# The HGRN loop of a two-layer diffusion backbone, regrouped into a two-stage pipeline over heads

## Chip, cores and metric

One core of a Trainium2 chip runs the whole kernel. The metric is device time in microseconds: the time before is the median of three runs, 1417.72 us (1417.47 to 1418.39). A profiled execution of the same kernel is the source of every duration below.

## What is computed

The reference is a two-layer backbone on 512 latent tokens of width 1024, with 256 context tokens. Layer 0 mixes tokens with a gated linear recurrence in two directions (HGRN2), layer 1 with a short convolution; each is followed by a squared-ReLU MLP. The part that the change touches is the recurrence, in 8 heads of 128 channels:

```python
parts = split(h @ w_in, 5)                 # forget gates of two directions, value, query, output gate
f = lb + (1 - lb) * sigmoid(parts[d])      # per direction d;  k = 1 - f,  g = log f
cum = cumsum(g)                            # within chunks of 64 tokens
o_inter = (q * exp(cum)) @ S
scores = tril((q * exp(cum - ref)) @ (k * exp(ref - cum)).T)
o = o_inter + scores @ v
S = exp(last) * S + (k * exp(last - cum)).T @ v     # the first S comes from the context tokens
y = rmsnorm(o_dir0 + o_dir1) * gnorm * silu(gate)
```

All of it is float32. A matrix product of the layers is made of three products of rounded halves (high with high, high with low, low with high).

## The kernel before

Channels lie on the partitions and tokens along the rows, 512 wide. Weights come in blocks of 1024 by 256, each in two halves (`load_half`): SP's queue loads a half, ScalarE rounds it (`whi`, L316), VectorE makes the rest (`wlo`, L317). Three such halves fit at a time (pool `wa`). One head goes through these steps:

- **Forget products** (`forget_steps`, `block_steps`, tile `ps_fl`): 48 matmuls of 512 columns for the two directions' gates of the latent tokens; 48 of 256 columns for the context tokens (`context_products`, `ps_fc`).
- **Gates** (`forget_gates`, `latent_sigmoid`, `context_sigmoid`): sigmoids on ScalarE into `k` and `kc`, and on VectorE a copy of the products plus a bias, `zb` (L737).
- **Operands** (`logs`, `latent_ops`): logarithms and exponentials on ScalarE, scans along the tokens and products on VectorE. They give the scaled keys and queries of both directions and the scaled context keys `kc`.
- **Recurrence** (`context_states`, `states`, `scores`, `recurrence`): transposes, context states (`ctr`, `cst`), states (`ktr`, `kv`, `S`), masked scores (`sc`, `scm`, `scs`) and the output `po`, then the sum of squares `oms`. These are short matmuls, each waiting for ScalarE or VectorE between steps.
- **Readout** (`readout`): output gate and normalisation into `yT`.

Two heads share the query block (`silu_steps(3, ...)`, tile `ps_p`), the output gate block (`p4`, also `ps_p`) and the value block (`value_products`, `psv`), each of the same size as a forget block or, for the values, 144 matmuls of 256 columns.

The loop goes over pairs of heads, A and B. In a pair the order of the text is: operands of A, values, recurrence of A, operands of B, gate block, recurrence of B. While a recurrence runs, an object `Fill` puts matmuls of the next forget block (or of the query block, or in the last head of the first half of the output projection, `out_steps`, `ps_woa`) between its short matmuls; the table `GAPS` says for each head how many go into each of seven gaps. `Fill.step` fixes the order of these matmuls on TensorE. So the operands of a head are made right ahead of its recurrence, and the products that stand in the text between them (values, gate block, the rest of a block) are what TensorE has meanwhile.

A scheduler places each instruction on its engine when its simulated inputs are ready, first by the order of the text; each engine then runs its list in order. `tables.switch` keeps the activations that need one ScalarE table together: sigmoids of one group, then logarithms and exponentials (`LOGEXP`), then sigmoids again. Product banks of PSUM: four for `mm_tile` (`ps_fl`, `ps_fc`, `ps_p`, `psv`, `ps_woa`), three for the short matmuls (`sm_tile`), one for `po` and `oms`.

`tick()` takes two of the 24 units of the layer's other modulation vectors: each unit is a load of 512 KB on SP's queue into one of two buffers and one VectorE step of 128 by 1024 (`acc`, L442, L444); every eighth ends with a rounding (`alo`, L455) and two matmuls (`adaps`). `tick` is called up to five times a pair, from the second pair on.

Before the last recurrence, `y_split` rounds the finished heads 0 to 3 (`y_hi`, `y_lo`, L229, L230), which `out_steps` multiplies.

Of the kernel before, what the change touches and what calls it, by code (L numbers as in the profile page):

```python
# [46 lines left out]
def dit_kernel(ctx, tc, x, c, ctx_in, c_ctx, ada_w, ada_b, norm1, norm2, norm_f, mlp_w1, mlp_w2,  # L47
# [309 lines left out]
    class Fill:  # L357


        def __init__(self, hd, *steps):  # L360
            self.gaps, self.steps, self.ins = iter(GAPS[hd]), steps, None

        def gap(self):

            n = next(self.gaps)
            for steps in self.steps:
                for ins in itertools.islice(steps, n):
                    self.step(ins)
                    n -= 1
# [7 lines left out]
        def finish(self, i=0):  # L377

            for _ in self.steps[i]:
                pass  # L380
# [260 lines left out]
    def context_sigmoid(z, hd):  # L641
        kc = ht("kc", f"kc_{hd}", 2 * CTX, 1)
        act_fn(kc, z, AF.Sigmoid)
        return kc

    def logs(zs, hd):
# [6 lines left out]
        for d in range(2):  # L653
            kk, z = zs[d][1]
            g = ht("g", f"g_{hd}_{d}", SEQ + 2, 2)
# [6 lines left out]
        for d in range(2):  # L662
# [4 lines left out]
            c_ = ht("c64", f"c64_{name}", SEQ, 3)  # L667
# [16 lines left out]
            e1 = ht("de", f"e1_{name}", SEQ, 4)  # L684
# [29 lines left out]
    def context_states(kc, hd, vc, fill):  # L714

        ps = sm_tile(f"ctr_{hd}")
        for t in range(4):
            ins = nc.tensor.transpose(ps[:, t * P:(t + 1) * P], kc[:, t * P:(t + 1) * P], ident)
            fill.step(ins)
            pins.setdefault(f"ctr{hd}", ins)  # L720
        fill.gap()
        kT = ht("kT", f"kcT_{hd}", 2 * CTX, 2)
        nc.scalar.copy(kT, ps)
        ps2 = sm_tile(f"cst_{hd}")
        for d in range(2):
            for t in range(2):
# [48 lines left out]
    def states(o, d, s0, v, name, fill):  # L775
        order = list(range(4) if d == 0 else range(3, -1, -1))
        ps = sm_tile(f"ktr_{name}")
        for i, n in enumerate(order[:3]):
            fill.step(nc.tensor.transpose(ps[:, i * P:(i + 1) * P], o["kp"][:, n * P:(n + 1) * P], ident))
# [15 lines left out]
    def recurrence(hd, ops, s0, v, fill):  # L795

        S = []
        for d in range(2):
            S.append(states(ops[d], d, s0[d], v, f"{hd}_{d}", fill))
            if d:  # L800
                fill.gap()
# [458 lines left out]
```

## Time and profile before

| | us |
|---|---|
| median of the runs | 1417.72 |
| profiled execution, its own time | 1422.73 |
| its span in the trace | 1420.8 |
| TensorE busy in the span | 1361.4 |
| VectorE busy | 910.9 |
| ScalarE busy | 578.7 |

In the trace PE is TensorE's matmul row and PEld its row of weight loads, DVE is VectorE, ACT ScalarE, POOL GpSimd, SP the queue that loads weights. L316 is line 316 of the kernel. Matmuls overlap each other, so one's duration is longer than the distance from its start to the next one's; that distance, here called the pitch, is what a matmul costs in a row of them. PEclk is the granted clock of TensorE as a share of 2.4 GHz; it takes two levels, 1.0 and 0.5 (1.2 GHz).

### The profile page before, as it was taken

To read this page: it belongs to the slowest core of one execution; us is meant where nothing else is said; L and a number is where in the kernel's file an instruction comes from. 1 tells how busy PE (TensorE), PEld (TensorE's weight loads), DVE (VectorE), ACT (ScalarE), POOL (GpSimd) and SP (SyncE) were. 2 spreads that over 40 slices of the span, in tenths; PEclk is the share of its full clock that TensorE was granted. 3 is DMA by queue.
4 is the path that set the end of the run, shared out by engine and by line. 5 is a ranking of instruction groups with operands and counts; after the bars stand their busy time and mean duration, and the time that the engine had idled before them with its cause. 6 is when DMAs were issued, how large, how long until landed. Compare 5 with 4: busy or idle time off the path is not lost.

```text
span 1420.8 us, 18668 instructions
## 1 busy us (share of the span) xinstructions
PE 1361.4 (96%) x7418; PEld 1162.3 (82%) x7418; DVE 910.9 (64%) x1378; ACT 578.7 (41%) x877; POOL 78.9 (6%) x87
## 2 busy tenths in 40 slices
PE   6998999999996989999999999999999999999997
PEld 4797897978885888888888889888889888888887
DVE  5695987878769697676565547544578544444536
ACT  6573447336545354242342434322244323132333
POOL 3000000000000210000000002000030100000000
PEclk9999999999997999999999999999999999999999
DMA  9713214423211316566555331333334532323211
GB/s 267 210 45 119 90 45 119 134 90 104 75 51 54 106 58 237 193 193 222 177 170 173 104 103 61 106 102 95 98 104 134 178 104 89 100 93 103 91 59 60
DMA packets 142267, 167.60 MB, mean 118 GB/s; under 512 B 6692, under 2 KB 121572, under 8 KB 142180
## 3 DMA queue, kind: packets, MB, share of 16 engines
q1 hardware_dynamic: 140964, 164.70, 36.4%
q0 software_dynamic: 1088, 1.65, 0.6%
q8 instruction: 58, 0.95, 0.3%
q14 instruction: 29, 0.24, 0.0%
q10 hardware_dynamic: 128, 0.05, 0.0%
HBM read 164.25 MB, written 2.14 MB: 117 GB/s over the span
## 4 chain that ended last, share of the span: by engine, by line
PE 76%; DVE 16%; DMA 3%; ACT 2%; issue 2%; SPq 0%; POOL 0%; DVEq 0%; ACTq 0%
PE ps_w L340 22%; PE ps_w L343 11%; PE ps_w2t L1199 4%; PE ps_w2t L1197 4%; PE ps_w2t L1198 4%; PE ps_fl L340 2%; DMA ada<-in_ada_w_dram 2%; PE ps_cvb L340 2%; PE ps_cwo L340 2%; PE ps_cvx L340 2%; PE ps_cvc L340 2%; PE ps_fc L340 1%; PE ps_p L340 1%; PE ps_fl L343 1%; PE ps_cvb L343 1%
## 5 line engine op out<-in xcount | busy, mean ns | idle before, releaser
L316 ACT CAST whi_w<-raw_w 128x1024 fp32r<-128x1024 f32 x128 | 134.2, 1053 | 279.3 <-PE ps_w L340 150.5
L317 DVE TENSOR_TENSOR wlo_w<-raw_w,whi_w 128x1024 fp32r<-128x1024 f32 x116 | 141.4, 1223 | 161.3 <-ACT whi_w L316 160.9
L340 PE MATMUL ps_w<-h_a_hi,whi_w 128*128 128x512 f32 (+1 forms) x576 | 207.5, 367 | 2.5 <-ACT h_a_hi L232 2.5
L340 PE MATMUL ps_w<-h_a_lo,whi_w 128*128 128x512 f32 x448 | 174.3, 389 | 0.0
L340 PEld LDWEIGHTS ps_w<-h_a_hi,whi_w 128*128 128x128 f32 x576 | 108.5, 188 | 21.1 <-ACT h_a_hi L232 2.9
L444 DVE SCALAR_TENSOR_TENSOR acc<-ada,cs,acc 128x1024 f32<-128x1024 f32 x70 | 89.8, 1283 | 49.0 <-DMA ada<-in_ada_w_dram 48.9
L343 PE MATMUL ps_w<-h_a_hi,wlo_w 128*128 128x512 f32 x448 | 119.7, 389 | 0.0
L1197 PE MATMUL ps_w2t<-whi_w,u_hi 128*128 128x512 f32 (+1 forms) x288 | 105.3, 366 | 0.0
L1198 PE MATMUL ps_w2t<-wlo_w,u_hi 128*128 128x512 f32 (+1 forms) x288 | 105.3, 366 | 0.0
L1199 PE MATMUL ps_w2t<-whi_w,u_lo 128*128 128x512 f32 (+1 forms) x288 | 105.2, 365 | 0.0
L340 PE MATMUL ps_w<-u_lo,whi_w 128*128 128x512 f32 (+1 forms) x288 | 103.3, 366 | 0.7 <-DVE u_lo L1069 0.7
L340 PE MATMUL ps_w<-u_hi,whi_w 128*128 128x512 f32 (+1 forms) x288 | 103.4, 366 | 0.0
L343 PEld LDWEIGHTS ps_w<-h_a_hi,wlo_w 128*128 128x128 f32 x448 | 84.1, 188 | 17.5
L340 PEld LDWEIGHTS ps_w<-h_a_lo,whi_w 128*128 128x128 f32 x448 | 84.1, 188 | 17.5
L1068 DVE TENSOR_TENSOR mr<-mr 128x512 f32<-128x512 f32 (+1 forms) x72 | 45.0, 630 | 45.5 <-ACT u_hi L1067 45.5
L1066 ACT ACTIVATE mr<-ps_w 128x512 f32<-128x512 f32 (+1 forms) x72 | 39.2, 545 | 80.0 <-PE ps_w L343 80.0
L343 PE MATMUL ps_w<-u_hi,wlo_w 128*128 128x512 f32 (+1 forms) x288 | 70.2, 365 | 0.0
L340 PEld LDWEIGHTS ps_w<-u_lo,whi_w 128*128 128x128 f32 x288 | 54.3, 189 | 10.0 <-DVE u_lo L1069 1.2
L340 PEld LDWEIGHTS ps_w<-u_hi,whi_w 128*128 128x128 f32 x288 | 54.3, 189 | 9.1
L1199 PEld LDWEIGHTS ps_w2t<-whi_w,u_lo 128*128 128x128 f32 x288 | 54.3, 189 | 8.8 <-issue 0.2
L1198 PEld LDWEIGHTS ps_w2t<-wlo_w,u_hi 128*128 128x128 f32 x288 | 54.3, 189 | 8.8
L1197 PEld LDWEIGHTS ps_w2t<-whi_w,u_hi 128*128 128x128 f32 x288 | 54.3, 189 | 8.7
(374 smaller groups left out, 3103.7 us busy)
## 6 DMA issues: line engine op xcount, KB each, us to landing
raw_w<-in_mlp_w_dram SPq DMA_DIRECT2D x128, 512.0 KB, 3.8
ada<-in_ada_w_dram SPq DMA_DIRECT2D x80, 512.0 KB, 4.7
adaw<-in_ada_w_dram SPq DMA_DIRECT2D x32, 256.0 KB, 5.5
raw_f<-in_hgrn_w_in_dram SPq DMA_DIRECT2D x32, 256.0 KB, 4.0
raw_p<-in_hgrn_w_in_dram SPq DMA_DIRECT2D x12, 512.0 KB, 3.5
raw_v<-in_hgrn_w_in_dram SPq DMA_DIRECT2D x8, 512.0 KB, 4.1
raw_cvb<-in_conv_w_in_dram SPq DMA_DIRECT2D x8, 512.0 KB, 3.6
raw_cwo<-in_conv_w_out_dram SPq DMA_DIRECT2D x8, 512.0 KB, 3.4
```

What stands on the lines that cost most here:

```text
L316: pins[name] = nc.scalar.copy(hi, raw)
L317: eng.tensor_tensor(out=lo, in0=raw, in1=hi, op=ALU.subtract)
L340: yield nc.tensor.matmul(ps, lhsT=w[i][:, k % KH, ms], rhs=rhs[k][j][:, c0:c1], start=(k == first and (i, j) == (0, 0)), stop=False)
L343: yield nc.tensor.matmul(ps, lhsT=w[late[0]][:, k % KH, ms], rhs=rhs[k][late[1]][:, c0:c1], start=False, stop=(k == last))
L444: ins = nc.vector.scalar_tensor_tensor(out=acc, in0=raw[:, 0, :], scalar=cs[:, j, 0:1], in1=acc, op0=ALU.mult, op1=ALU.add)
L1066: nc.scalar.activation(r, ps, AF.Relu)
L1068: nc.vector.tensor_tensor(out=r, in0=r, in1=r, op=ALU.mult)
L1197: nc.tensor.matmul(ps, lhsT=u[k][0][:, tk], rhs=whi[:, kk, c0:c1], start=(k == 0), stop=False)
L1198: nc.tensor.matmul(ps, lhsT=u[k][0][:, tk], rhs=wlo[:, kk, c0:c1], start=False, stop=False)
L1199: nc.tensor.matmul(ps, lhsT=u[k][1][:, tk], rhs=whi[:, kk, c0:c1], start=False, stop=(k == KT - 1))
```

## The change

- The loop goes over heads instead of pairs. In the text, the recurrence of head h comes first with the forget products of head h+2 as its fill (latent and context products, both through `Fill` now), then the operands of head h+1, then the gates of head h+2. Behind the fill stand the query block (even h) or the values (odd h) of the next pair.
- The output gate blocks of pairs 1 to 3 are kept back: two of them are the fill of head 6, the third follows it. The gate of a head is then multiplied into `yT` after its normalisation (`gate_y`).
- Ahead of the loop stand the operands of head 0, the forget products of head 1 and the values of pair 0.
- `GAPS` is one row of five lengths in microseconds for all heads; a matmul of 512 columns counts 0.227, one of 256 counts 0.118. In a recurrence all transposes come first, then the context states, both directions' states, then the scores.
- `zb` and the scaling of `k` are made by ScalarE (Identity with a per-partition bias, or scale and bias) instead of VectorE.
- `kl` and `ql` are written over `k`. Buffers: `g` 4 instead of 2, `k` 4 instead of 3, `c64` 4 instead of 3, `kc` 2 instead of 1, `de` is split into `qt` (3) and `kt` (4). The scratch for GpSimd's DMAs is set to 4096 bytes.
- `tick(2)` (four units) is called once a head, from head 0 on. The readout of head h-1 stands after the scores of head h, ahead of their sum `scs`.

```diff
-GAPS = ((0, 9, 4, 6, 5, 18, 9),
-        (66, 9, 5, 6, 4, 6, 0),
-        (0, 9, 4, 6, 2, 12, 12),
-        (22, 20, 10, 6, 4, 14, 18),
-        (0, 9, 9, 6, 2, 12, 14),
-        (18, 24, 5, 10, 6, 19, 14),
-        (0, 9, 4, 6, 2, 12, 12),
-        (30, 20, 4, 6, 4, 18, 7))
+GAPS = (3.2, 2.4, 2.4, 3.6, 4.6)
...
+        def __init__(self, *steps):
+            self.steps, self.ins = itertools.chain(*steps), None
+
+        def gap(self, us):
+
+            while us > 0:
+                got = next(self.steps, None)
+                if got is None:
+                    return
+                self.step(got[0])
+                us -= got[1]
...
-        kc = ht("kc", f"kc_{hd}", 2 * CTX, 1)
+        kc = ht("kc", f"kc_{hd}", 2 * CTX, 2)
...
-            g = ht("g", f"g_{hd}_{d}", SEQ + 2, 2)
+            g = ht("g", f"g_{hd}_{d}", SEQ + 2, 4)
...
-            c_ = ht("c64", f"c64_{name}", SEQ, 3)
+            c_ = ht("c64", f"c64_{name}", SEQ, 4)
...
-            e1 = ht("de", f"e1_{name}", SEQ, 4)
+            e1 = ht("qt", f"e1_{name}", SEQ, 3)
...
-            nc.vector.tensor_scalar(out=r["kk"], in0=r["kk"], scalar1=col(lb1n, d, hd), scalar2=col(lb1, d, hd),
-                                    op0=ALU.mult, op1=ALU.add)
+            nc.scalar.activation(r["kk"], r["kk"], AF.Identity, scale=col(lb1n, d, hd), bias=col(lb1, d, hd))
...
-        kk = ht("k", f"k_{hd}_{d}", SEQ, 3)
+        kk = ht("k", f"k_{hd}_{d}", SEQ, 4)
         act_fn(kk, z, AF.Sigmoid)
-        zb = ht("de", f"zb_{hd}_{d}", SEQ, 4)
-        nc.vector.tensor_scalar(out=zb, in0=z, scalar1=col(lbig, d, hd), scalar2=None, op0=ALU.add)
+        zb = ht("kt", f"zb_{hd}_{d}", SEQ, 4)
+        nc.scalar.activation(zb, z, AF.Identity, bias=col(lbig, d, hd))
...
+    def recurrence(hd, ops, kc, v, vc, fill, between):
+        orders = [list(range(4)), list(range(3, -1, -1))]
+        ps = sm_tile(f"ctr_{hd}")
+        for t in range(4):
+            fill.step(nc.tensor.transpose(ps[:, t * P:(t + 1) * P], kc[:, t * P:(t + 1) * P], ident))
+        kcT = ht("kcT", f"kcT_{hd}", 2 * CTX, 1)
+        nc.scalar.copy(kcT, ps)
+        kT = []
+        for d in range(2):
+            ps = sm_tile(f"ktr_{hd}_{d}")[:, 0:3 * P]
+            for i, n in enumerate(orders[d][:3]):
+                fill.step(nc.tensor.transpose(ps[:, i * P:(i + 1) * P], ops[d]["kp"][:, n * P:(n + 1) * P], ident))
+            kT.append(ht("kT", f"kT_{hd}_{d}", 3 * P, 2))
+            nc.scalar.copy(kT[d], ps)
+        fill.gap(GAPS[0])
+        ps = sm_tile(f"cst_{hd}")
+        for d in range(2):
+            for t in range(2):
+                fill.step(nc.tensor.matmul(ps[:, d * P:(d + 1) * P], lhsT=kcT[:, (2 * d + t) * P:(2 * d + t + 1) * P],
+                                           rhs=vc[:, t, :], start=(t == 0), stop=(t == 1)))
+        s0 = ht("S0", f"S0_{hd}", 2 * P, 1)
+        nc.scalar.copy(s0, ps[:, 0:2 * P])
         S = []
         for d in range(2):
-            S.append(states(ops[d], d, s0[d], v, f"{hd}_{d}", fill))
-            if d:
-                fill.gap()
-            scores(ops[d], d, hd, fill)
-        fill.gap()
+            order = orders[d]
+            ps = sm_tile(f"kv_{hd}_{d}")
+            for i, n in enumerate(order[:3]):
+                fill.step(nc.tensor.matmul(ps[:, i * P:(i + 1) * P], lhsT=kT[d][:, i * P:(i + 1) * P], rhs=v[:, n, :],
+                                           start=True, stop=True))
+            S.append({order[0]: s0[:, d * P:(d + 1) * P]})
+            for i, n in enumerate(order[:3]):
+                s = ht("S", f"S_{hd}_{d}_{i}", P, 6)
+                nc.vector.scalar_tensor_tensor(out=s, in0=S[d][n], scalar=ops[d]["e128"][:, n:n + 1],
+                                               in1=ps[:, i * P:(i + 1) * P], op0=ALU.mult, op1=ALU.add)
+                S[d][order[i + 1]] = s
+        fill.gap(GAPS[1])
+        scores(ops[0], 0, hd, fill)
+        fill.gap(GAPS[2])
+        scores(ops[1], 1, hd, fill)
+        between()
         scs = tmp.tile([P, SEQ], F32, tag="nt", name=f"scs_{hd}", bufs=3)
         nc.vector.tensor_tensor(out=scs.rearrange("p (n t) -> p n t", t=P), in0=scm[0], in1=scm[1], op=ALU.add)
+        fill.gap(GAPS[3])
...
+        fill.gap(GAPS[4])
...
+    def gate_y(hd, gate):
+        nc.vector.scalar_tensor_tensor(out=yT[hd], in0=yT[hd], scalar=gnq[:, hd:hd + 1], in1=gate, op0=ALU.mult,
+                                       op1=ALU.mult)
+    def readout(hd, pr, gate=None):
+        if gate is not None:
+            gate_y(hd, gate)
         r = rsqrt(pr, SEQ, f"o{hd}", P)
+        nc.vector.tensor_tensor(out=yT[hd], in0=yT[hd], in1=r, op=ALU.mult)
...
+        for ins in block_steps(w, got["ps"], h0):
+            yield ins, 0.227
+        got["c"] = mm_tile(f"ps_fc{hd}")
+        for d in range(2):
+            for h in range(2):
+                for ins in mm_steps(got["c"][:, d * CTX:(d + 1) * CTX], w[h], mslice(d), hc,
+                                    range(h * KH, (h + 1) * KH), 0, CTX, 0, KT - 1):
+                    yield ins, 0.118
...
+    hold_ada[0] = False
+    qs, gs, got, z = {}, {}, {}, {}
+    for part, b, into in ((3, "q", qs), (4, "g", gs)):
+        for mi in range(2):
+            into[mi] = silu(part, 0, mi, first_ps[(b, mi)])
+    z[0] = forget_gates(0, {"ps": [first_ps[("f", d)] for d in range(2)], "c": first_ps["c"]})
+    tables.switch(LOGEXP)
+    def operands(hd):
+        r, kc = logs(z.pop(hd), hd)
+        return [latent_ops(r[d], qs[hd], d, f"{hd}_{d}") for d in range(2)], kc
+    ops = {0: operands(0)}
+    Fill(forget_steps(1, got)).finish()
+    vl, vc = value_products(0)
+    tables.switch()
+    z[1] = forget_gates(1, got)
+    tables.switch(LOGEXP)
+    prs = {}
+    def gates(hp, pss):
+        for mi in range(2):
+            t = silu(4, hp, mi, pss[mi])
+            if hp < 3:
+                gate_y(2 * hp + mi, t)
+            else:
+                gs[2 * hp + mi] = t
+    for hd in range(HEADS):
+        hp, m = divmod(hd, 2)
+        got = {}
+        if hd == HEADS - 1:
+            for k in range(KH):
+                y_split(k)
+            fill = Fill(out_steps())
+        elif hd == HEADS - 2:
+            fill = Fill(silu_steps(4, 1, got), silu_steps(4, 2, got))
+        else:
+            fill = Fill(forget_steps(hd + 2, got))
+        def between():
+            if hd > 0:
+                readout(hd - 1, prs[hd - 1], gs.get(hd - 1))
+        o, kc = ops.pop(hd)
+        prs[hd] = recurrence(hd, o, kc, vl[:, :, m * P:(m + 1) * P], vc[:, :, m * P:(m + 1) * P], fill, between)
+        fill.finish()
+        if hd == HEADS - 1:
+            break
+        ops[hd + 1] = operands(hd + 1)
+        tables.switch()
+        if hd < HEADS - 2:
+            z[hd + 2] = forget_gates(hd + 2, got)
+            if m == 0:
+                Fill(silu_steps(3, hp + 1, got)).finish()
                 for mi in range(2):
+                    qs[hd + 2 + mi] = silu(3, hp + 1, mi, got[3, hp + 1][mi])
+            else:
+                vl, vc = value_products(hp + 1)
         else:
+            for p_ in (1, 2):
+                gates(p_, got[4, p_])
+            Fill(silu_steps(4, 3, got)).finish()
+            gates(3, got[4, 3])
+        tick(2)
         tables.switch(LOGEXP)
...
     with tc.high_priority():
+        readout(HEADS - 1, prs[HEADS - 1], gs[HEADS - 1])
...
-    nc = _bacc.Bacc("TRN2", target_bir_lowering=False, num_devices=1)
+    nc = _bacc.Bacc("TRN2", target_bir_lowering=False, num_devices=1, dynamic_dma_scratch_size=4096)
```

The deleted lines of the old loop, of `states` and of `context_states` are left out; their code is in the listing above.

## Rows read from the trace of the kernel before

**Rows 1.** Stretch 86 to 481 us: length, then busy us of PE, PEld, DVE, ACT, POOL, PEclk, DMA.

```profile
86.00:481.00 395.00, 367.41 (x2351) 324.14 (x2350) 308.96 (x531) 198.38 (x308) 6.53 (x27) 0.96 0.27 85
```

**Rows 2.** Groups by line and shape, TensorE, 86 to 481 us: busy, mean ns, idle before.

```profile
L340 PE MATMUL ps_fl<-h_hi,whi_f 128*128 128x512 f32 x112 | 46.7, 417 | 0.1
...
L827 PE MATMUL oms<-osq,ones 128*128 128x512 f32 x2 | 1.0, 592 | 0.0
```

**Rows 3.** TensorE in order of time: start us, us, what, idle before.

```profile
86.09 0.28 PE L892 MATMUL psv<-wlo_v,hc_hi 128*128 128x256 f32 x1
...
86.80 0.28 PE L892 MATMUL psv<-wlo_v,hc_hi 128*128 128x256 f32 x1
...
410.02 0.39 PE L809 MATMUL po<-c,S 128*128 128x128 f32 x2
...
411.37 0.39 PE L809 MATMUL po<-c,S 128*128 128x128 f32 x2
...
449.35 0.63 PE L340 MATMUL ps_woa<-y_hi,whi_woa 128*128 128x512 f32 x1
449.78 0.63 PE L340 MATMUL ps_woa<-y_hi,wlo_woa 128*128 128x512 f32 x1
...
454.35 0.39 PE L340 MATMUL ps_woa<-y_hi,wlo_woa 128*128 128x512 f32 x1
454.58 0.39 PE L340 MATMUL ps_woa<-y_hi,whi_woa 128*128 128x512 f32 x1
```

**Rows 4.** Waits of TensorE, 86 to 481 us: total us, times, longest.

```profile
PE ps_woa L343 <- DVE y_lo L230: 12.4, 1, 12.4
PE ctr L718 <- DVE kc L711: 5.4, 3, 2.0
PE sc L768 <- DVE S L790: 4.3, 2, 4.0
PE adaps L461 <- DVE alo L455: 3.1, 1, 3.1
PE sc L768 <- DVE scm L773: 1.0, 1, 1.0
PE psv L891 <- DVE gc L694: 0.8, 1, 0.8
PE ps_p L340 <- DVE gc L694: 0.4, 1, 0.4
```

**Rows 5.** Waits of VectorE, 86 to 481 us.

```profile
DVE wlo_p L317 <- ACT whi_p L316: 14.9, 7, 3.8
...
DVE g L666 <- ACT g L110: 9.0, 7, 1.9
DVE acc L444 <- DMA ada<-in_ada_w_dram: 7.2, 8, 1.5
```

**Rows 6.** VectorE in order of time: operands of one head, and what follows them.

```profile
276.83 0.69 DVE L666 TENSOR_TENSOR g<-zb,g 128x512 f32<-128x512 f32 x1
...
288.02 0.69 DVE L711 TENSOR_TENSOR kc<-kc,gc 128x512 f32<-128x512 f32 x1
...
295.66 0.69 DVE L220 TENSOR_SCALAR nt_o<-oms 128x512 f32<-128x512 f32 x1
```

**Rows 7.** Groups by line and shape, VectorE, 86 to 481 us.

```profile
L737 DVE TENSOR_SCALAR zb<-ps_fl,lbig 128x512 f32<-128x512 f32 x14 | 10.4, 749 | 5.6 <-ACT k L110 5.6
...
L702 DVE TENSOR_SCALAR k<-k,lb1n,lb 128x512 f32<-128x512 f32 x16 | 8.7, 544 | 0.0
```

**Rows 8.** Groups by line and shape, ScalarE, 86 to 481 us.

```profile
L93 ACT ACT_TABLE_LOAD x11 | 14.1, 1283 | 0.2
L110 ACT ACT_TABLE_LOAD x10 | 12.8, 1283 | 0.2
...
L110 ACT ACTIVATE g<-k,lb,lb 128x512 f32<-128x512 f32 x16 | 12.2, 811 | 0.1
...
L110 ACT ACTIVATE y_o<-oms,eps_t 128x512 f32<-128x512 f32 x8 | 5.5, 687 | 1.4 <-PE oms L827 1.4
```

More of the change, by code (lines that the diff above doesn't have):

```diff
@@ L375, in step, with finish @@
             self.ins = first if last is None else last
-        def finish(self, i=0):
-            for _ in self.steps[i]:
-                pass
+        def finish(self):
+            self.gap(1e9)
     def mslice(mi):
@@ L860, in silu_steps @@
         w = load_block(f"p{part}_{hp}", wcols(part, hp))
-        got["ps"] = [mm_tile(f"ps_p{part}_{hp}") for _ in range(2)]
-        yield from block_steps(w, got["ps"], h0)
+        got[part, hp] = [mm_tile(f"ps_p{part}_{hp}") for _ in range(2)]
+        for ins in block_steps(w, got[part, hp], h0):
+            yield ins, 0.227
     def out_steps():
@@ L869, in out_steps @@
                 ps = mm_tile(f"ps_woa{i}")
-                yield from mm_steps(ps, w, mslice(mi), y2, range(KH), 0, SEQ, 0, KH - 1, fresh=True)
+                for ins in mm_steps(ps, w, mslice(mi), y2, range(KH), 0, SEQ, 0, KH - 1, fresh=True):
+                    yield ins, 0.227
                 with tc.high_priority():
@@ L904, in y_split @@
         y2.append(pr)
-    late = []
-    qn, fn = {}, {}
-    for hp in range(4):
-        hold_ada[0] = hp == 0
-        A, B = 2 * hp, 2 * hp + 1
-        qg = {}
-        if hp == 0:
-            for part, b in ((3, "q"), (4, "g")):
+    hold_ada[0] = False
[4 more added lines that the diff above has]
+    z[0] = forget_gates(0, {"ps": [first_ps[("f", d)] for d in range(2)], "c": first_ps["c"]})
@@ L927, in dit_kernel @@
-        oA = [latent_ops(rA[d], qg[(3, 0)], d, f"{A}_{d}") for d in range(2)]
-        vl, vc = value_products(hp)
-        fn = {}
-        fill = Fill(A, forget_steps(B, fn))
-        fill.gap()
-        s0 = context_states(kcA, A, vc[:, :, 0:P], fill)
-        for f in late:
-            f()
-        late = []
-        tick()
-        prA = recurrence(A, oA, s0, vl[:, :, 0:P], fill)
-        tables.switch()
-        fill.finish()
-        zB = forget_gates(B, fn["ps"], fn["w"])
-        tick()
@@ L942, in dit_kernel @@
-        tables.switch(LOGEXP)
-        rB, kcB = logs(zB, B)
-        oB = [latent_ops(rB[d], qg[(3, 1)], d, f"{B}_{d}") for d in range(2)]
-        if hp > 0:
-            tables.switch()
-            block_products(load_block(f"p4_{hp}", wcols(4, hp)), h0, silu_part(4, hp, qg), f"p4_{hp}", 0, SEQ)
-            tick()
-            tables.switch(LOGEXP)
-        if hp == 3:
-            for hd in range(KH):
-                y_split(hd)
-        qn, fn = {}, {}
-        fill = Fill(B, *([silu_steps(3, hp + 1, qn), forget_steps(B + 1, fn)] if hp < 3 else [out_steps()]))
@@ L955, in dit_kernel @@
-        fill.gap()
-        s0 = context_states(kcB, B, vc[:, :, P:], fill)
-        readout(A, prA, qg[(4, 0)])
-        prB = recurrence(B, oB, s0, vl[:, :, P:], fill)
-        late = [lambda B=B, prB=prB, g=qg[(4, 1)]: readout(B, prB, g)]
-        if hp < 3:
-            tables.switch()
-    fill.finish()
+                    qs[hd + 2 + mi] = silu(3, hp + 1, mi, got[3, hp + 1][mi])
+            else:
+                vl, vc = value_products(hp + 1)
+        else:
+            for p_ in (1, 2):
+                gates(p_, got[4, p_])
+            Fill(silu_steps(4, 3, got)).finish()
+            gates(3, got[4, 3])
```

104 lines of the change are left out of this document (16 added, 88 removed).

## The prediction

> **What bounds the kernel now.** I first looked at the busy time of each engine by stretch, to find the stage that the change touches: from the first value product (86 us) to the start of the second half of the output projection (481 us) TensorE is the busiest with 367 of 395 us, VectorE has 309, ScalarE 198 [rows 1]. In what follows the stage the code is the same, so the whole question is how far these 395 us lie above what TensorE must do.
>
> A busy share doesn't answer that, since matmuls overlap. The order of time gives the pitch: 0.23 us for 512 columns (454.35 to 454.58), 0.118 for 256 (86.09 to 86.80 is six), 0.1125 for 128 (410.02 to 411.37 is twelve) [rows 3]; for 64 columns I take half of that, 0.056, an estimate. The groups give the counts [rows 2] (the first and the last of 32 groups stand there): 748 of 512 columns (336 `ps_fl`, 288 `ps_p`, 96 `ps_woa`, 16 `oms`, 12 `adaps`), 912 of 256 (576 `psv`, 336 `ps_fc`), 560 of 128 (128 `sc`, 96 `kv`, 192 `po`, 64 `cst`, 48 `ktr`, 32 `ctr`), 128 of 64. That is 172.0 + 107.6 + 63.0 + 7.2 = **350 us of matmuls; 45 us are lost**.
>
> Where they go: the waits of TensorE add up to 27.4 us, all on VectorE [rows 4]. The other 18 are mostly the lower clock behind those waits. The granted clock is 0.96 on average [rows 1], and behind the longest wait the pitch is 0.43 us (449.35 to 449.78), the lower of the two levels, and 0.23 again by 454.35 [rows 3]. So a microsecond of wait costs 45/27.4 = 1.64 us. By place: the last head with its rounded halves `y_lo` 12.4, context keys that come late three times 5.4, the scores that wait for `S` 4.3, `adaps` 3.1, the rest 2.2.
>
> The Trainium skill ("Perfetto Trace Analysis", Identifying the Most-Contended Engine) says that matmul busy time is a poor measure of headroom and that the share of weight loads is a good one. Here the busy row would leave 28 us and the load row 395 - 324 = 71 us [rows 1]. The trace agrees with the first half only: the pitches put the room at 45, in between.
>
> **The change part by part.** *The work on TensorE* stays: the same matmuls in another order. Per head, from the pitches: recurrence (63.0 + 7.2 + 3.7)/8 = 9.2 us, forget products 11.0 + 5.7, a query or gate block 11.0, values 17.0, half the output projection 22.1. Head h of the loop takes 9.2 + 16.7 + 11.0 = 36.9 us for even h, 42.9 for odd h, 42.2 for head 6, 31.3 for head 7; ahead of it stand 16.7 + 17.0 = 33.7 us.
>
> *Operands a head earlier.* VectorE makes one head's operands in 18.8 us (276.83 to 295.66), the context keys 11.2 us in [rows 6]. Before, TensorE covered that with one block of 11 or 17 us, and the keys came late three times [rows 4]. Now a whole turn of 37 to 43 us lies between gates and recurrence. That removes the 5.4 us on `kc`, 0.8 and 0.4 on `gc`: with the clock 6.6 x 1.64 = 10.8 us. At the start the operands of head 0 have 33.7 us instead of 17.
>
> *VectorE gives two steps to ScalarE.* `zb` costs VectorE 0.749 us, `k` 0.544 [rows 7], each twice a head: 2.6 a head, 20.7 in all (16 x 1.293). On ScalarE, `zb` has one per-partition operand, as the logarithm with a bias (0.687), `k` two, as the logarithm with scale and bias (0.811) [rows 8]: 24.0 us more. The tables are switched about 17 instead of 21 times: 4 x 1.28 = 5.1 us less [rows 8]. ScalarE goes from 198 to 217 of 350 us and hides it; if it didn't, the 19 us would be the price.
>
> The Trainium skill ("ScalarE: Activation LUTs", Rules for kernel authors) says that additions and multiplications belong on VectorE. The rows agree for `k` (0.811 against 0.544) and not for `zb` (0.687 against 0.749); by the rule the move alone loses 3 us of engine time. Since VectorE is the fuller engine here, my sum counts it as a gain of slack.
>
> *VectorE's new load.* (309.0 - 20.7)/8 = 36.0 us a head. To it come waits that the new order need not remove: for rounded weights 14.9, for logarithms 9.0, for `acc`'s loads 7.2, together 31 or 3.9 a head [rows 5]. 39.9 fits into an odd turn (42.9) and not into an even one (36.9): 3.0 us short, three times, so 9 us if nothing carries over, 0 if odd turns lend their spare 3. I take 5, nearer the middle, as the operands may run ahead by a turn.
>
> *The recurrence's own waits.* The five gaps are 2.4 to 4.6 us; what they must cover is a copy by ScalarE or one or two steps of VectorE, each under 1.3 us, plus what is queued ahead of them. The readout's five or six steps now stand ahead of `scs`, some 4 us of VectorE at about the 0.69 of a row of 512 (its first step, [rows 6]) against a gap of 3.6. Before, scores waited once for `scm`, 1.0 us [rows 4]. I keep 3 us with the clock for eight heads; bounds 0 and 8 (one of it a head).
>
> *`tick(2)`.* Each tick issues four loads of 512 KB on SP's queue into two buffers: the third and fourth wait for VectorE's `acc`, and weight loads are queued behind them. VectorE waits for `acc`'s load 8 times, 7.2 us [rows 5], and `S`, queued behind one such step, cost TensorE 4.0; `adaps` waited 3.1 for `alo` once in three [rows 4]. Nothing in the change removes either. I keep one of them with its clock, 6 us; bounds 0 and 2 x (4.0 + 3.1) x 1.64 = 23.
>
> *The last heads.* Before head 7, VectorE made operands and then the four `y_lo`; TensorE had 11 us of other work and waited 12.4, some 20 us with the clock [rows 3, 4]. Now the operands of head 7 have 42.2 us of products beside them, but VectorE also makes the six kept gates there (10 steps at about the 0.75 of `zb`, of which a head's average holds some 3: 5 us more): 41 against 42.2, and `out_steps` begins in the first gap of head 7, so any rest shows. I keep 4 us; bounds 0 and 20.
>
> *Priced at nothing:* larger buffers, `kl` and `ql` in place. The smaller scratch meets only GpSimd's few loads, the last of them behind products of the second MLP; 0, and if that cover failed, two loads late by the longest wait for a load in the rows, 1.5 us [rows 5]: 3.
>
> **Sum.** Kept: 5 + 3 + 6 + 4 = 18. Removed: 45 - 18 = **27 us**. The profiled span goes from 1420.8 to 1394. The profiled execution (1422.7) lies 5.0 us above the median of the runs; I carry that over, and the median goes from 1417.7 to **1391**.
>
> **The rivals.** *Full cover.* All waits vanish, as TensorE has 350 us against VectorE's 288 + 31: 1417.7 - 45 = 1373. For it speaks that sum; against it that the waits of `acc` and of `y_lo` have causes the change leaves. 0.16.
>
> *More than full cover.* If only the weight loads bounded TensorE (324 us [rows 1]), a denser order would also shorten the pitch: 1417.7 - 71 = 1347. Against it stands the pitch of 0.23 us in the densest stretches [rows 3]; 0.02. The Trainium skill's measure in "Perfetto Trace Analysis" is what gives this case.
>
> *VectorE sets the pace.* Every wait on TensorE is for VectorE [rows 4]; if its order of work is as full of holes as before, the stage shrinks only by what was taken from it, 20.7 us: 1397. 0.15.
>
> *The last stall stays* as it was: the 20 us remain instead of 4, 1407. In the text `y_split` still stands behind the operands and now behind the gates too. 0.08.
>
> *Slower: the product banks.* After the forget products of head h+2, three of four banks wait for sigmoids, and `tables.switch` puts these behind every exponential of head h+1's operands. If VectorE does all its other work of the turn first (36.0 - 18 = 18 us), the keys come 18 + 11 = 29 us into the turn, and a table load, a sigmoid and an Identity later (1.28 + 0.69 + 0.69, the sigmoid taken as the logarithm with one operand [rows 8]) a bank at 31.7. TensorE wants it at 9.2 + 16.7 + 2.8 = 28.7: 3.0 us a head, 6.9 with the 3.9 of holes. Times 1.64 and seven heads, 34 to 79 us against the 45 lost now. It decides from 3.9 us a head; at the middle, 5, it costs 57 - 45 = 12: 1430. For it: the readout and `tick` stand ahead. Against it: operands can start in the turn before, and a stalled TensorE gives VectorE time. 0.11. That the scheduler doesn't make the pipeline at all (no change, 1418) gets 0.04.
>
> **How the numbers follow.** Forecast 0.44, the rivals 0.16, 0.02, 0.15, 0.08, 0.11 and 0.04. A measurement tells 0.2% (3 us) here. Faster: 0.44 + 0.16 + 0.02 + 0.15 + 0.08 less a little for the upper tail of the kept terms = 0.82; same 0.06; slower 0.12. The range goes from 1371 (full cover and 1 to 2 us less at the entry to the output projection) to 1412, the forecast with 21 us more of kept stalls (their bounds sum to 60 but won't meet), which leaves out the slower case and no change.
>
> **What would show it.** Right: no wait for `kc` or `gc`; the stage near 368 us with a clock of 0.98 or more; `zb` and `k` on ScalarE at 0.69 and 0.81 us; VectorE near 288 us in it. Wrong: `ps_p` or `psv` waiting for ScalarE's `k` or `zb` (banks), a wait for `y_lo` above 8 us (last stall), waits for operands in even heads of over 3 us (VectorE's pace).

## The result, and the profile after

The changed kernel takes **1397.8 us** (median of 4 runs, 1396.4 to 1399.8) where the kernel before, on the same chip, takes 1418.1 (4 runs, 1417.5 to 1421.2): a ratio of 0.9854 [0.9835, 0.9873], 20 us faster. The forecast was 1391, so the direction was right and 7 of the 27 us did not come. The profiled execution has 1398.2 us of its own time and a span of 1396.5; before it had 1422.7 and 1420.8.

The stage now runs from 85.7 to 457 us. Its row in the view by stretches, with the same columns as [rows 1]:

```profile
85.70:457.00 371.30, 359.91 (x2351) 320.99 (x2350) 292.50 (x503) 211.00 (x336) 6.65 (x26) 0.99 0.29 90
```

It has lost 24 of its 395 us; 371.3 stands against a forecast of 368 and against the 350 us of matmuls that the pitches gave. VectorE went from 309 to 292.5 (forecast 288) and ScalarE from 198 to 211 (forecast 217), and TensorE's granted clock from 0.96 to 0.99. Behind the stage nothing changed: from its end to the end of the span it is 1396.5 - 457 = 939.5 us, before 1420.8 - 481 = 939.8.

The waits of TensorE in the stage (total, times, longest), to be read against [rows 4]:

```profile
PE ktr L759 <- ACT row L455: 7.2, 3, 3.0
PE po L796 <- DVE scs L789: 2.2, 1, 2.2
PE psv L886 <- DVE wlo_v L310: 1.4, 1, 1.4
PE psv L885 <- ACT vl L890: 0.5, 1, 0.5
```

Every wait of [rows 4] is gone: `y_lo` 12.4, `kc` 5.4, `S` 4.3, `adaps` 3.1, `gc`. Of the four in their place the largest is `ktr` for ScalarE's `row`, three times. It is not a wait for data, since `ktr` doesn't read `row`. ScalarE in order of time at the first of the three (start, us, what, and in brackets the idle time before it), then TensorE:

```profile
203.69 1.03 ACT L309 CAST whi_f<-raw_f 128x1024 fp32r<-128x1024 f32 x1
204.63 0.36 ACT L890 COPY vl<-psv 128x256 f32<-128x256 f32 x1
204.89 1.05 ACT L309 CAST whi_f<-raw_f 128x1024 fp32r<-128x1024 f32 x1
205.84 1.04 ACT L309 CAST whi_p<-raw_p 128x1024 fp32r<-128x1024 f32 x1
206.78 0.37 ACT L890 COPY vl<-psv 128x256 f32<-128x256 f32 x1
207.05 1.05 ACT L455 COPY row<-adaps 1x512 f32<-1x512 f32 x2
208.00 0.57 ACT L754 COPY kcT<-ctr 128x512 f32<-128x512 f32 x1
```

```profile
204.06 0.60 PE L752 MATMUL ctr<-ident,kc 128*128 128x128 f32 x4
207.67 1.54 PE L759 MATMUL ktr<-ident,g 128*128 128x128 f32 x6 [3.02 <-ACT row L455]
208.87 0.78 PE L333 MATMUL ps_fl<-h_hi,whi_f 128*128 128x512 f32 x1
209.44 0.63 PE L333 MATMUL ps_fl<-h_lo,whi_f 128*128 128x512 f32 x1
209.87 0.63 PE L333 MATMUL ps_fl<-h_hi,whi_f 128*128 128x512 f32 x1
```

The two `adaps` of a modulation vector and `ctr` fill the three short-lived banks (`sm_tile`). `ktr` needs one of them back, and the copies that free them stand in ScalarE's list behind three roundings of 1.04 us and two value copies. TensorE is past `adaps` when `ctr` starts at 204.06, and `row` starts at 207.05. Then TensorE is 3.0 us idle, and the products behind it start at the lower of the two clock levels (209.44 to 209.87 is 0.43 us a piece).

The other wait, `scs`, comes from further up in VectorE's list:

```profile
306.36 1.28 DVE L437 SCALAR_TENSOR_TENSOR acc<-ada,cs,acc 128x1024 f32<-128x1024 f32 x1 [4.78 <-DMA ada<-in_ada_w_dram]
307.56 0.34 DVE L780 SCALAR_TENSOR_TENSOR S<-S,e,kv 128x128 f32<-128x128 f32 x1
...
312.43 1.28 DVE L437 SCALAR_TENSOR_TENSOR acc<-ada,cs,acc 128x1024 f32<-128x1024 f32 x1
313.63 0.71 DVE L744 COPY_PREDICATED scm<-mu,sc 128x512 f32<-128x512 uint8 x1
314.38 0.69 DVE L789 TENSOR_TENSOR scs<-scm,scm 128x512 f32<-128x512 f32 x1
```

A step of `acc` waits 4.8 us for its load, with `S`, both `scm` and `scs` of the recurrence queued behind it. Such waits have grown in the stage. Before, they were 10.9 us: the last line of [rows 5] (7.2, 8 times) and one for the first step of a vector, which [rows 5] leaves out:

```profile
DVE acc L442 <- DMA ada<-in_ada_w_dram: 3.7, 1, 3.7
```

After, they are 30.6 us:

```profile
DVE acc L437 <- DMA ada<-in_ada_w_dram: 26.0, 11, 5.3
DVE acc L435 <- DMA ada<-in_ada_w_dram: 4.6, 2, 2.5
```

The two steps that moved, in ScalarE's groups by shape (busy, mean ns, idle before), cost about what the forecast took (0.811 and 0.687):

```profile
L695 ACT ACTIVATE k<-k,lb,lb1n 128x512 f32<-128x512 f32 x16 | 12.4, 811 | 0.0
...
L710 ACT ACTIVATE zb<-ps_fl,lbig 128x512 f32<-128x512 f32 x14 | 9.7, 694 | 0.0
```

### The profile page after: what moved, and what is told of

The parts are those of the page before. It is cut to its first block, busy times and chain, and to the rows that moved or that the text cites. A ratio compares the mean times of both kernels' runs of the same rounds, so it can differ in the third digit from the quotient of the medians.

```text
span 1396.5 us, 18630 instructions
## 1 busy us (share of the span) xinstructions
PE 1353.6 (97%) x7418; PEld 1160.5 (83%) x7418; DVE 890.8 (64%) x1346; ACT 591.8 (42%) x905; POOL 79.1 (6%) x87
## 4 chain that ended last, share of the span: by engine, by line
PE 75%; DVE 16%; DMA 3%; ACT 3%; issue 3%; SPq 0%; POOL 0%; DVEq 0%; ACTq 0%
PE ps_w L333 22%; PE ps_w L336 11%; PE ps_w2t L1203 4%; PE ps_w2t L1202 4%; PE ps_w2t L1204 4%; PE ps_p L333 3%; DMA ada<-in_ada_w_dram 3%; PE ps_cvb L333 2%; PE ps_cwo L333 2%; PE ps_cvc L333 2%; PE ps_cvx L333 2%; PE ps_p L336 1%; PE ps_fl L333 1%; PE ps_woa L333 1%; PE ps_cvb L336 1%
## 5 line engine op out<-in xcount | busy, mean ns | idle before, releaser
L437 DVE SCALAR_TENSOR_TENSOR acc<-ada,cs,acc 128x1024 f32<-128x1024 f32 x70 | 89.7, 1281 | 67.7 <-DMA ada<-in_ada_w_dram 67.5
```

The lines of the kernel that those rows point to most:

```text
L437: ins = nc.vector.scalar_tensor_tensor(out=acc, in0=raw[:, 0, :], scalar=cs[:, j, 0:1], in1=acc, op0=ALU.mult, op1=ALU.add)
```

## The experiments

Each ratio is the kernel's time over that of the kernel before in the same set of runs. Kernels of different experiments are compared by these ratios.

**1. The kernel before, once more.** Why was its profiled execution 5 us above the median, and may that offset be carried over to another kernel?

> The kernel before, unchanged, profiled a second time. Theory A (the 5 us by which the first profiled execution lay above the median of the runs were waits in the HGRN stage that differ from execution to execution, so they must not be carried over to the changed kernel): the second profiled execution lies nearer to 1418, with a stage of 388 to 392 us instead of 394.9 and shorter waits of TensorE in it. Theory B (profiling itself costs a fixed 5 us): again 1422 to 1423 and a stage of 394 to 395 us.

This profiled execution took 1414.3 us, 8.4 less than the first. Its stage, and the one of its waits above 3 us that differs from [rows 4] (`y_lo` and `kc` stand there with the same numbers):

```profile
84.00:471.00 387.00, 360.65 (x2353) 319.26 (x2352) 309.11 (x531) 198.42 (x309) 6.55 (x27) 0.98 0.28 87
```

```profile
PE sc L768 <- DVE S L790: 3.0, 2, 2.6
```

The waits add up to 26.2 us where [rows 4] has 27.4, the stage is 8 us shorter, and the granted clock is 0.98 where [rows 1] has 0.96. With levels of 1.0 and 0.5, these means are some 32 us of 395 and 15 of 387 at the lower level; half of the difference is 8 us. Between 296 and 304 us the clock is 0.57 in the first execution, and in the second it is 1.00 from 290 to 310. So the offset is no fixed cost of a profiled execution: it is how long the lower clock lasts behind nearly the same waits, and that differs from one execution to the next. Over 17 runs of this job the kernel before has a median of 1418.2 (1414.6 to 1424.8).

**2. Only the last stall of before.** Kernel before, the four early splits put ahead in the schedule.

```diff
+            with tc.high_priority():
-            for hd in range(KH):
-                y_split(hd)
+                for hd in range(KH):
+                    y_split(hd)
```

> The kernel before, with the rounded halves of heads 0 to 3 made ahead of the operands of head 7 on VectorE, and nothing else. Theory A (the 12.4 us wait for y_lo is only the order of work on VectorE; it makes up most of the gain of the whole change): the wait falls under 3 us, the time falls by 12 to 17 us to 1401 to 1406. Theory B (VectorE is full there, so what is made earlier makes the operands of head 7 late): the wait moves to ctr or sc in head 7, the time falls by less than 5 us.

1413.1 us (8 runs, 1410.6 to 1416.9), ratio 0.9957 [0.9934, 0.9979]: at the edge of theory B. The 12.4 us on `y_lo` are gone, but `sc` now waits 6.0 us for `S` (3 times, before 4.3) and `ps_woa` 3.3 for `xT`, which is new: part of the wait moved to later steps of VectorE. Taking away the biggest wait of [rows 4] alone gave some 6 us (0.43%), not the 20 that I had put on it with its clock.

**3. Only the two steps moved to ScalarE**, in the kernel before.

```diff
-            nc.vector.tensor_scalar(out=r["kk"], in0=r["kk"], scalar1=col(lb1n, d, hd), scalar2=col(lb1, d, hd),
-                                    op0=ALU.mult, op1=ALU.add)
+            nc.scalar.activation(r["kk"], r["kk"], AF.Identity, scale=col(lb1n, d, hd), bias=col(lb1, d, hd))
...
-        nc.vector.tensor_scalar(out=zb, in0=z, scalar1=col(lbig, d, hd), scalar2=None, op0=ALU.add)
+        nc.scalar.activation(zb, z, AF.Identity, bias=col(lbig, d, hd))
```

> The kernel before, with only zb and the scaling of k moved from VectorE to ScalarE. Theory A (VectorE's amount of work sets the pace): the stage shrinks by most of the 20.7 us taken from VectorE, 1397 to 1405. Theory B (the order of the work sets it, the amount doesn't): less than 6 us, 1412 to 1419, with VectorE at about 289 us in the stage and the waits for y_lo and kc within 3 us of what they were.

1419.9 us (10 runs), ratio 1.0002 [0.9986, 1.0019]: nothing, as theory B has it for the time. Against theory B the waits for `y_lo` and `kc` did not stay (1.2 and 1.8 us). But all waits of TensorE in the stage still add up to 25.7 us, now partly for ScalarE:

```profile
PE ps_woa L340 <- ACT y_hi L229: 8.5, 1, 8.5
PE psv L890 <- ACT vc L895: 7.7, 7, 2.5
PE ps_p L340 <- DVE gc L694: 3.3, 1, 3.3
```

VectorE's busy time in the stage fell from 309 to some 291 us and the time stood still. That speaks against the rival "VectorE sets the pace", though ScalarE took on as much (198 to 217 us), and two of the waits are now for it. Experiment 4 tries the rival without that.

**4. The same two steps back on VectorE**, in the changed kernel (the diff of 3, the other way).

> The changed kernel, with zb and the scaling of k back on VectorE. Theory A (the pipeline needs VectorE's slack: turns of even heads are 36.9 us against 36.0 us of work and 3.9 of waits, and 2.6 more a head don't fit): 8 to 20 us slower than the changed kernel, 1406 to 1418, with waits for operands at the start of odd heads. Theory B (the pipeline has slack enough in the turns of odd heads): within 3 us of 1398.

1404.1 us (4 runs), ratio 0.9883 [0.9851, 0.9916] against 0.9854 [0.9835, 0.9873] of the changed kernel. The time lies between the two theories, and the intervals overlap, so what the move gives inside the pipeline (some 4 us by the ratios) isn't settled. VectorE is busy for 309 us in the stage, as before the change, and the kernel is still 1.2% faster than before: the amount of VectorE's work did not set the pace. What the profile adds is `psv` waiting 3.4 us (3 times) for VectorE's `zb`: the value products wait for a bank whose forget gate is not yet read.

**5. `adaps` in the long banks**, changed kernel.

```diff
-            ps = sm_tile(f"adaps_{l}_{v}_{hf}")
+            ps = (mm_tile if l == 0 and v < 5 else sm_tile)(f"adaps_{l}_{v}_{hf}")
```

> The changed kernel, with the two matmuls of a modulation vector (adaps) in the four product banks instead of the three banks of the short matmuls. Theory A (the 7.2 us for which ktr waits for the copies of adaps are a lack of banks for short matmuls): these waits go, and with the lower clock behind them the time falls by 7 to 12 us to 1386 to 1391. Theory B (ScalarE's list is the limit: ktr's banks come free but cst or kv then waits for kcT and kT behind the same roundings): the waits move to cst or kv and the time falls by less than 3 us.

1390.9 us (5 runs, 1386.1 to 1397.7), ratio 0.9808 [0.9779, 0.9836], 0.46% or 6.5 us below the changed kernel; the two intervals just touch. No `ktr` waits any more; `scs` grew from 2.2 to this:

```profile
PE po L796 <- DVE scs L789: 7.0, 3, 2.8
```

So the 7.2 us were a matter of the bank. The profiled execution is the slowest of the five (1397.7 us, 6.8 above the median), so its 7.0 us on `scs` need not be those of the others.

**6. Two ticks apart**, changed kernel: one `tick()` ahead of the operands and one at the end in place of `tick(2)`.

```diff
+        tick()
         ops[hd + 1] = operands(hd + 1)
...
-        tick(2)
+        tick()
```

> The changed kernel, with two units of the modulation vectors called ahead of the operands and two at the end of each turn, instead of four at the end. Theory A (four loads into two buffers make VectorE wait: 30.6 us for acc against 10.9 before, and through it the 2.2 us of po for scs): VectorE's wait for acc falls below 18 us, the wait of po goes, the time falls by 3 to 5 us. Theory B (the scheduler places the units by its own readiness, so the place in the text does little): VectorE's wait stays at 25 to 35 us and the time within 2 us of the changed kernel.

1401.9 us (5 runs), ratio 0.988 [0.9858, 0.9902]: no gain, theory B. `acc` still waits 29.4 us for loads (24.8 at L437; 30.6 in the changed kernel), and `po` 4.8 for `scs`. The place in the text did not spread the steps: in VectorE's list six steps of `acc` start between 302.7 and 319.9 us, in the changed kernel four between 299.5 and 312.4. So this run doesn't tell what a real spacing does.

**7. Both of them** (5 and 6).

> The changed kernel with both edits: adaps in the product banks and the units called two by two. If each does what its theory A says: 1382 to 1388, a stage of 356 to 360 us. If only the banks count: as the run with the banks alone, 1386 to 1391.

1392.5 us (4 runs), ratio 0.9813 [0.9787, 0.9838]; `scs` 6.9. The bank acts: 6 and 7 differ in it alone, by 0.67% or 9.5 us, and their intervals lie apart. The ticks, placed so, do nothing that shows.

**8. The operands late.** Does the gain come from making operands a head ahead? Changed kernel; the first operand step of head h+1 is ordered on VectorE behind `sqlo`, VectorE's last step in the recurrence of head h (not behind the readout, which comes a head later).

```diff
-            nc.vector.tensor_tensor(out=gi, in0=z, in1=gi, op=ALU.min)
+            ins = nc.vector.tensor_tensor(out=gi, in0=z, in1=gi, op=ALU.min)
+            if rec_end[0] is not None:
+                tc.add_manual_dep(ins.ins, rec_end[0].ins.name, NOSYNC, reason="order")
...
-            nc.vector.tensor_tensor(out=lo, in0=osq, in1=hi, op=ALU.subtract)
+            rec_end[0] = nc.vector.tensor_tensor(out=lo, in0=osq, in1=hi, op=ALU.subtract)
```

> The changed kernel, but with VectorE's list held to the old turn: the first step of the operands of head h+1 stands behind the last step of the readout of head h, so they are no longer made beside the recurrence of head h. ScalarE's two steps, the kept gate blocks and the order of TensorE's products stay. Theory A (the gain comes from the operands made one head ahead: TensorE finds kc, k and gc done when it gets to them): waits of TensorE for operands come back, 15 us or more in the stage, VectorE's busy time stays near 292 us, and the time is 1405 to 1425. Theory B (the gain comes from the kept gate blocks and from the forget products two heads ahead; when VectorE makes the operands matters little): under 5 us of waits for operands, and the time is 1395 to 1402.

1443.8 us (4 runs), ratio 1.0172 [1.0144, 1.0199]: some 45 us slower than the changed kernel, and slower than before. Theory A has the mechanism; its size was too small (1405 to 1425). Stage, waits of TensorE, and VectorE at one hand-over:

```profile
86.00:506.00 420.00, 376.23 (x2363) 332.93 (x2362) 297.56 (x505) 213.64 (x339) 7.25 (x26) 0.93 0.26 81
```

```profile
PE ktr L763 <- DVE g L730: 24.7, 5, 6.4
PE psv L889 <- ACT vc L894: 10.9, 3, 3.8
```

```profile
237.92 0.69 DVE L793 TENSOR_TENSOR scs<-scm,scm 128x512 f32<-128x512 f32 x1
245.32 0.69 DVE L809 TENSOR_TENSOR sqlo<-osq,sqhi 128x512 fp32r<-128x512 f32 x1 [6.71 <-ACT sqhi L808]
245.93 1.29 DVE L661 TENSOR_TENSOR g<-zb,g 128x512 f32<-128x512 f32 x2
```

VectorE's busy time is nearly that of the changed kernel. But it now idles 6.7 us ahead of `sqlo`, and the chain of operands starts only then; TensorE waits for `g` (24.7 us) and for banks (10.9), and its granted clock falls to 0.93. The experiment is harsher than the kernel before, where operands ran beside one block of products and the gates of the next head did not stand behind them. So 45 us is not the gain of the pipeline; the run shows that, with this order of TensorE's products, the head of lead is needed. The waits for `S`, `scm` and `y_lo` stay away here too, but TensorE stands still for 44 us elsewhere, so the run doesn't tell which part of the change removed those.

**9. One load per vector.** Kernel of 5, but of the eight loads of each vector of layer 0 only the first, so the vectors are not those of the reference.

```diff
-        raw = rawp.tile([P, 1, D], F32, tag="araw", name=f"ada_{l}_{v}_{j}", bufs=2)
-        dma_w(raw, ada_w[l][:, v * D:(v + 1) * D].rearrange("(p j) c -> p j c", j=KT)[:, j:j + 1, :])
+        if j == 0 or l > 0:
+            stt["raw"] = rawp.tile([P, 1, D], F32, tag="araw", name=f"ada_{l}_{v}_{j}", bufs=2)
+            dma_w(stt["raw"], ada_w[l][:, v * D:(v + 1) * D].rearrange("(p j) c -> p j c", j=KT)[:, j:j + 1, :])
+        raw = stt["raw"]
```

> The kernel with the adaps products in the long banks, and of the eight loads of each vector of layer 0 only the first; the other seven products of acc read that same tile, so the vectors are not the reference's. Theory A (the stall of po for scs comes from acc, which waits for its load in VectorE's list ahead of S, scm and scs): acc's waits for loads fall from some 25 us to under 8, po's waits for scs from 7.0 us to under 2.5, and the stage of 369.8 us gets 4 us or more shorter, the time 1379 to 1387. Theory B (scs is late because VectorE has the recurrence's and the next operands' steps in one list, loads or not): po still waits 4 us or more, and the time stays at 1388 to 1394.

1384.2 us (4 runs, 1382.5 to 1384.9), ratio 0.975 [0.9732, 0.9769], another 0.58% or 8.2 us below 5, and the intervals lie apart; theory A. Its stage, what is left of `acc`'s waits, and `scs`:

```profile
84.30:443.00 358.70, 355.80 (x2352) 318.23 (x2351) 291.48 (x504) 210.95 (x337) 6.58 (x26) 1.00 0.21 63
```

```profile
DVE acc L437 <- DMA ada<-in_ada_w_dram: 3.8, 2, 2.1
```

```profile
PE po L798 <- DVE scs L791: 0.2, 1, 0.2
```

VectorE does as much as in the changed kernel (291.5 us) and DMA less (a share of 0.21 for 0.29). The run can't tell whether a part of the 8 us is due to the emptier DMA queue rather than to `acc`'s waits. A part lies outside the stage: the profiled span without its stage is 1022.0 us here and 1026.1 in kernel 5.

**10. The units of `acc` one by one.** Kernel of 5; each unit is ordered behind a step after which VectorE has time: `scs`, `sqlo`, and the last operand step of each direction.

```diff
+    def unit(after):
+        ada_after[0] = after
+        if ada_queue:
+            ada_unit(*ada_queue.pop(0))
+        ada_after[0] = None
...
+        if 0 < hd < HEADS - 1:
+            unit(ins)
...
+        if not name.startswith("0_"):
+            unit(ins)
...
-        tick(2)
```

> The kernel with the adaps products in the long banks, and the four units of acc of each head no longer in a bunch at the head's end but one by one: behind scs, behind the last step of the readout, and behind the last operand step of each direction, so that each load has longer to come and none stands ahead of scs. Theory A (acc's waits ahead of scs make po's stall): po's waits for scs fall from 7.0 us to under 3, acc's waits to under 12 us, and the time is 1380 to 1388. Theory B (acc's waits are harmless, scs is late for another reason): po still waits 5 us or more for scs and the time is 1388 to 1394; were the loads only moved against the weight loads, ps_p or psv would wait in their place.

**1390.3 us** (5 runs, 1386.8 to 1390.6), ratio 0.9787 [0.9767, 0.9807]. It is faster than before and than the changed kernel. The waits are theory A's (`scs` 0.3, `acc` 5.3), the time lies in theory B's range:

```profile
85.70:449.00 363.30, 357.12 (x2353) 318.50 (x2353) 293.07 (x504) 211.93 (x337) 6.17 (x26) 1.00 0.30 93
```

```profile
DVE acc L437 <- DMA ada<-in_ada_w_dram: 5.3, 2, 3.5
```

```profile
219.55 0.69 DVE L797 TENSOR_TENSOR scs<-scm,scm 128x512 f32<-128x512 f32 x1
220.16 1.28 DVE L437 SCALAR_TENSOR_TENSOR acc<-ada,cs,acc 128x1024 f32<-128x1024 f32 x1
```

With the same loads as the changed kernel, `acc` waits 5.3 us for them instead of 30.6, `po` waits 0.3 for `scs`, and the stage is 8 us shorter than the changed kernel's. But against kernel 5, which has the bank and not the order, the ratios overlap (0.9787 against 0.9808). Two new waits, `adaps` for `ahi` (2.0 us) and `cst` for `kcT` (1.8), take back some of it. What placing the units adds to the bank isn't settled, and so the 8 us of experiment 9 aren't shown to be the price of `acc`'s waits.

**11. One kept gate block given back.** Changed kernel; the gate block of heads 2 and 3 in the turn of head 4, not beside head 6.

```diff
-            fill = Fill(silu_steps(4, 1, got), silu_steps(4, 2, got))
+            fill = Fill(silu_steps(4, 2, got))
...
+                if hp == 2:
+                    Fill(silu_steps(4, 1, got)).finish()
+                    gates(1, got[4, 1])
...
-            for p_ in (1, 2):
-                gates(p_, got[4, p_])
+            gates(2, got[4, 2])
```

> The changed kernel with one kept gate block given back: the gate block of heads 2 and 3 is no longer made beside head 6's recurrence but in the turn of head 4, so that head 6 has 31 us of products (9.2 + 11.0 + 11.0) over the operands of head 7 instead of 42. Theory A (the kept gate blocks are what covers the last heads): a wait for y_lo, xT, kc or k of 5 us or more appears at the end of the loop, with the lower clock behind it, and the time is 1404 to 1412. Theory B (the operands made one head ahead are cover enough, the second kept block adds nothing): no new wait above 2 us at the end of the loop and the time stays at 1395 to 1401.

1398.7 us (6 runs), ratio 0.9863 [0.9837, 0.9889]: as the changed kernel, theory B. All waits of TensorE in the loop:

```profile
PE ktr L759 <- ACT row L455: 7.0, 3, 2.8
PE psv L886 <- DVE wlo_v L310: 1.5, 1, 1.5
PE po L796 <- DVE scs L789: 0.8, 1, 0.8
```

No wait for `y_lo` comes back: one of the two kept blocks is cover enough for head 6. Whether it needs that one wasn't tried.

## Why the prediction was right or wrong

**The bound: right. The floor: 6 us too low.** TensorE bounds the stage, and no version went below the 350 us from pitches and counts. But in experiment 9 the clock is 1.00 throughout and the waits of TensorE add up to 2.9 us, and the stage still takes 358.7: 355.8 us are matmuls. The 6 us more stand at the scores. In the changed kernel:

```profile
306.91 1.05 PE L740 MATMUL sc<-e,zb 128*128 128x128 f32 x8
307.89 0.68 PE L742 MATMUL sc<-k 128*64 128x64 f32 x8
308.50 0.50 PE L333 MATMUL ps_fl<-h_lo,whi_f 128*128 128x512 f32 x1
308.84 0.40 PE L333 MATMUL ps_fl<-h_hi,whi_f 128*128 128x512 f32 x1
```

From 306.91 to 308.84 is 1.93 us, where the pitches give 1.58 (eight of 0.1125, eight of 0.056, one of 0.23); the block product behind the scores alone takes 0.34. Sixteen such places, two a head, with 0.35 us more each make 5.6 us. So of the 45 us that I called lost some 6 were never to be had, and a microsecond of wait cost 39/27.4 = 1.4 rather than 1.64.

The Trainium skill ("Perfetto Trace Analysis", Identifying the Most-Contended Engine) takes, beside the share of the peak rate, the busy share of weight loads as the measure of headroom. After the change that row leaves 371 - 321 = 50 us, and a floor of 356 leaves 15; experiment 10, with its clock at 1.00, has 318.5 us of loads in a stage of 363.3. Here the measurement decides against the share. The rival "more than full cover" that rested on it did not come.

**Operands a head earlier: right, and the heart of it.** No wait for `kc` or `gc` is left, and with the lead taken away TensorE waits for `g`, another of the operands (experiment 8). The lead can be read off the lists. Before, `kc` was done 0 to 2 us ahead of the transposes that read it in heads 0 to 6: the one that starts at 288.02 us in [rows 6] is read here:

```profile
290.00 0.60 PE L718 MATMUL ctr<-ident,kc 128*128 128x128 f32 x4
```

After, it is done 20 to 47 us ahead. Head 7, where the longest wait of before was:

```profile
376.73 0.67 DVE L703 TENSOR_TENSOR kc<-kc,gc 128x512 f32<-128x512 f32 x1
...
420.64 2.49 DVE L223 TENSOR_TENSOR y_lo<-yT,y_hi 128x512 fp32r<-128x512 f32 x4
```

```profile
424.63 0.60 PE L752 MATMUL ctr<-ident,kc 128*128 128x128 f32 x4
```

The operands of head 7 no longer stand right ahead of `y_lo`, and `y_lo` is done before TensorE begins the head. What removed the waits for `S`, `scm` and `adaps` (8.4 of the 27.4 us) wasn't tried by itself: the order within the recurrence, the gaps and the buffers changed together with the lead.

**Two steps to ScalarE: costs right, effect smaller than the argument suggested.** 0.811 and 0.694 us as taken. The forecast counted the move as slack for VectorE. Alone the move gives nothing (experiment 3); inside the pipeline some 4 us by the ratios, not settled (experiment 4). The Trainium skill ("ScalarE: Activation LUTs", Rules for kernel authors) would have additions and multiplications stay on VectorE; no run here shows a loss by moving them.

**Even turns, 5 us, and the last heads, 4 us: both came out at nothing.** There is no wait for operands and none for `y_lo`, nor with 11 us less cover (experiment 11). In both steps I compared VectorE's load of a turn with the length of that turn; that the lead lets VectorE draw on the turn before is the likely reason, not a tested one.

**The recurrence's own waits, 3 us: nothing of their own.** The one wait for `scs` (2.2) was expected behind the readout's steps; the list at 306 to 314 us shows `acc` and its load ahead of it, and experiments 9 (without the loads) and 10 (with `acc` put behind `scs`) take the wait away.

**`tick(2)`, 6 us: sized too small.** I named both its parts, loads and `adaps`, and kept one of two stalls as before had them. After the change these two make 9.4 of the 11.3 us that TensorE waits (`row` and `scs`). Measured by taking them out, the banks of `adaps` cost 6.5 us (experiment 5; 9.5 between 6 and 7). For the loads there is no one price: 8.2 us without them (experiment 9, a part of it outside the stage), and nothing clear of noise with the units put where VectorE has time (experiment 10). The bound of 23 held. Two things were missed. First, `adaps` was taken as something that waits, not as something that holds two of three banks until ScalarE gets to a copy. Secondly, with operands ahead, VectorE gets to `acc` earlier than its load: 30.6 us of waits where before had 10.9. With the operands late again (experiment 8) it is 8.8.

**The sum: near, in part by luck.** Above a floor of 356 us the stage keeps 371.3 - 355.8 = 15.5 us, where I kept 18: more for `tick(2)`, less for the other three. That the terms together came so near is luck, since their errors have opposite signs. The stage came out 3 us above the forecast because the floor was 6 too low. That is some 3 of the 7 us that did not come.

**The offset, 5 us: wrong.** The other 4 of the 7 us are the offset of the profiled execution that I carried over. After the change the profiled execution lies 0.4 us from the median. Experiment 1 shows why: before's first execution had more of the lower clock behind its waits than the second, and the median lies between the two. Those microseconds stood already in the 45 that were lost, and I took them off a second time. Reckoned from the median, with some 40 lost, the same kept 18 give 1418 - 40 + 18 = 1396; with the floor put right as well, 1418 - 34 + 18 = 1402.

**The rivals.** Full cover (1373) did not come: its floor was too low, and `tick(2)` left waits. Experiment 9, with 2.9 us of waits and the full clock, gets to 1384. "VectorE sets the pace" hit the time (1397) by luck: its reason is wrong, since with the two steps back on VectorE most of the gain stays (experiment 4). The last stall did not stay. The product banks did not stall in the changed kernel (0.5 and 1.4 us on `psv`); with `zb` on VectorE they begin to (3.4 us, experiment 4), and with late operands they do (10.9, experiment 8).

## What to carry to other kernels

When a pipeline gives an engine a head of lead, the next thing to look at is what else stands in its list: a step that waits for a transfer now waits longer, because the engine reaches it sooner, and all that is queued behind it is late. A wait whose releaser is a copy that the waiting instruction doesn't read is a wait for a bank; count who holds the few banks, and for how long, in the list of the engine that frees them. Make the sum of a forecast against a median execution, or against several profiled ones, since the same waits can cost different times. Add to a floor of pitches what the changes between kinds of products cost, read from a place where nothing waits.

## What the runs showed of the hardware

Two executions of the same program with nearly the same waits of TensorE (27.4 and 26.2 us) had a mean granted clock of 0.96 and 0.98 in the stage, and the stage took 395 and 387 us. A copy out of a single partition is no cheaper than one out of 128: `row`, 1x512, took ScalarE 0.569 us on average (6 of them), `kcT`, 128x512, 0.580 (8). A block product of 512 columns right behind the 64-column products of the scores had a pitch of 0.34 us (308.50 to 308.84), where 0.23 is usual.
